# Adding the last square of thirteen norms on TensorE instead of VectorE

## The chip, the cores and the metric
The kernel runs on one core of a Trainium2 chip. A core has engines that work side by side, each with its own instruction stream: TensorE (PE in the rows; PEld is its weight load), VectorE (DVE), ScalarE (ACT), GpSimd (POOL), and SyncE (SP), which issues most transfers. The metric is the time of one execution in microseconds (us), as the device takes it.

## The reference
Two layers of a diffusion backbone work on 512 latent tokens of 1024 channels (and, in layer 0, on 256 context tokens as keys and values). Layer 0 mixes tokens by differential attention, layer 1 by a Hyena long convolution; a squared-ReLU MLP follows each. Every sub-layer has a norm over the channels before it and one behind it:

```
def rms_norm(x, g, eps=NORM_EPS):
    y = x * lax.rsqrt(jnp.mean(x * x, axis=-1, keepdims=True) + eps)
    return y * g

u = modulate(rms_norm(h, norm_mix_pre[i]), mod[0], mod[1])
y = mixer(u)                                   # attention or Hyena
h = h + mod[2] * rms_norm(y, norm_mix_post[i])
v = modulate(rms_norm(h, norm_mlp_pre[i]), mod[3], mod[4])
h = h + mod[5] * rms_norm(square(relu(v @ w_in)) @ w_out, norm_mlp_post[i])
```

## The kernel before, in words
Activations lie transposed: a tile has 128 channels on the partitions and tokens along its row, so 1024 channels are eight tiles. From the end of attention on, the tokens go in two halves of 256. Large products are split in three: a float32 operand becomes a rounded part (hh, uh, whi, wxhi) and a rest (hl, ul, wlo, wxlo), and each product is three matmuls, lines 308 to 310. The weights' parts are made on the chip: ScalarE casts a raw tile (line 286), VectorE or GpSimd subtracts (line 287).

A norm over channels for one half is this. As each of the eight tiles appears, ScalarE squares it (line 373, `nsq`, three buffers). `squares` adds them up: the sum with squares 2 to 5 on GpSimd, with 6 to 8 on VectorE (`NPOOL` = 5, line 382, `nacc`). `rstd` then sums over the partitions by TensorE: for each of the two blocks of 128 tokens a matmul whose loaded operand is the block of `nacc` and whose streamed one is a column of ones (line 349, into `ps_s`). A chain of small operations takes the inverse root: `rs_v` on VectorE (353), `rs_z` on ScalarE (329), five on VectorE (332 to 336). TensorE transposes the result to all partitions (line 362, `ps_bc`, "the broadcast"). It is used in one of two ways. `residual` multiplies y by it and adds the gain times y to the hidden state hT (lines 971 and 972, eight times each), and squares hT for the next norm as it goes. `prenorm` makes the modulated, split input of the next layer (lines 984 to 986, `nt`, `uh`, `ul`, eight times each).

There are fourteen such norms, counted here in order of time: 1 to 4 behind layer 0's attention (half 0: behind the mixer, before the MLP; then half 1 the same), 5 to 8 at the end of layer 0's MLP and before Hyena, 9 to 12 behind Hyena's output projection, 13 and 14 at the end of layer 1's MLP, one for each half. While a norm's chain runs, TensorE works on other matmuls of 256 columns of the other half or the next product (`ps_h`, in `halves`).

The last norm has a form of its own: `squares(..., two=True)` (set in `mlp`, line 1062, for layer 1's half 1) does not add the eighth square but returns the sum of seven and the eighth, and `rstd` runs a matmul for each of the two parts into the same column of `ps_s`.

The order of the instructions on each engine is not that of the code. A list scheduler places them by its own estimates of times and by priorities (`PRI`, by part of the program: `css` for the sum over channels, `cbc` for the broadcast, `res`, `pre`, `wload` and so on). A change of one instruction can so move others on all engines.

Of the kernel before, what the change touches and what calls it, by code (L numbers as in the profile page):

```python
# [20 lines left out]
KT = D // P  # L21
T = 512
TC = 256
HT = T // 2
# [232 lines left out]
class K:  # L257
# [104 lines left out]
                nc.tensor.transpose(bc[:, b * P:(b + 1) * P], z[:, b:b + 1].to_broadcast([P, P]), self.ident)  # L362
        return bc[:, 0:n]

    def squares(self, pool, n, two=False):


        nc = self.nc
        st = {"n": 0}

        def add(src):
            sq = pool.tile([P, n], F32, tag="nsq", name="nsq", bufs=3)
            nc.scalar.activation(sq, src, AF.Square)
            st["n"] += 1
            if st["n"] == 1:
                st["acc"] = sq
            elif two and st["n"] == KT:
                return st["acc"], sq
            else:
                eng = nc.vector if st["n"] > NPOOL else nc.gpsimd  # L380
                acc = pool.tile([P, n], F32, tag="nacc", name="nacc", bufs=2) if st["n"] == 2 else st["acc"]
                eng.tensor_add(acc, st["acc"], sq)
                st["acc"] = acc
            return st["acc"]
        return add
# [632 lines left out]
    def mlp(self, layer, u, after, chores=()):  # L1018

        nc, ap, y = self.nc, self.ap, self.y  # L1020
        uh, ul = u
        chores = iter(chores)
        for g in range(4):
            hid = [(self.hp.tile([P, T], F32R, tag="hh", name="hh"), self.hp.tile([P, T], F32R, tag="hl", name="hl"))
                   for _ in range(8)] if g == 0 else []
            if g == 0:
                ws = [self.wload(ap[f"w1_{layer}"][mt], f"w1f{layer}", True if layer else "xxxwwwxx"[mt])
                      for mt in range(8)]
                for h in range(2):
                    hs = slice(HT * h, HT * h + HT)  # L1030
                    yield h
                    self.halves(ws, lambda k: (uh[:, k], ul[:, k]),
                                lambda mt, ps: self.hidden(ps, hid[mt][0][:, hs], hid[mt][1][:, hs]), h,
                                HG[f"w1f{layer}"])
            else:
                for mt in range(8):
                    w = self.wload(ap[f"w1_{layer}"][8 * g + mt], f"w1_{layer}", True)
                    ps = self.pp.tile([P, T], F32, tag="mm", name="ps_1")
                    self.mm3(ps, [(*self.lin(w, k), uh[:, k], ul[:, k]) for k in range(KT)])
                    hid.append((self.hp.tile([P, T], F32R, tag="hh", name="hh"),  # L1040
                                self.hp.tile([P, T], F32R, tag="hl", name="hl")))
                    self.hidden(ps, *hid[mt])
                    next(chores, None)
            if g < 3:
                self.part = f"{layer}."
                for mt in range(8):
                    w = self.wload(ap[f"w2_{layer}"][g, mt], f"w2_{layer}", True)
                    ps = self.pp.tile([P, T], F32, tag="mm", name="ps_2")
                    self.mm3(ps, [(*self.lin(w, k), *hid[k]) for k in range(KT)])
                    if g == 0:  # L1050
                        nc.scalar.copy(y[:, mt], ps)
                    else:
                        nc.vector.tensor_add(y[:, mt], y[:, mt], ps)  # L1053
                    next(chores, None)
            else:
                for _ in chores:
                    pass
                self.part = "ef"[layer] + "."
                ws = [self.wload(ap[f"w2_{layer}"][g, mt], f"w2l{layer}", True) for mt in range(8)]
                for h in range(2):  # L1060
                    hs = slice(HT * h, HT * h + HT)
                    sq = self.squares(self.tp, HT, two=layer == 1 and h == 1)
                    res = {}

                    def evac(mt, ps):
                        nc.vector.tensor_add(y[:, mt, hs], y[:, mt, hs], ps)
                        res["acc"] = sq(y[:, mt, hs])
                    self.halves(ws, lambda k: hid[k], evac, h, HG[f"w2l{layer}"])
                    after(h, res["acc"])
# [280 lines left out]
```

## Time and profile before

| | |
|---|---|
| time, median of three runs | 1447.67 us (1447.07 to 1450.67) |
| the profiled execution: its time, its span | 1445.6 us, 1443.6 us |
| TensorE busy | 1390.7 us, 96% |
| VectorE busy | 922.8 us, 64% |
| ScalarE busy | 646.6 us, 45% |
| GpSimd busy | 181.6 us, 13% |

TensorE is busy for 90% or more of every slice of 36 us from the fourth of forty slices to the last but one. A row of a timeline below gives the start in us from the span's beginning, the busy time, engine, source line, operation, out<-in, shape and count of instructions that follow each other, and in brackets how long the engine had been idle before it and what ended that. Busy times of instructions that overlap are longer than the distance from one to the next; that distance is called the pitch here.

### The profile page before, as it was taken

To read this page: it belongs to the slowest core of one execution; us is meant where nothing else is said; L and a number is where in the kernel's file an instruction comes from. 1 tells how busy PE (TensorE), PEld (TensorE's weight loads), DVE (VectorE), ACT (ScalarE), POOL (GpSimd) and SP (SyncE) were. 2 spreads that over 40 slices of the span, in tenths; PEclk is the share of its full clock that TensorE was granted. 3 is DMA by queue.
4 is the path that set the end of the run, shared out by engine and by line. 5 is a ranking of instruction groups with operands and counts; after the bars stand their busy time and mean duration, and the time that the engine had idled before them with its cause. 6 is when DMAs were issued, how large, how long until landed. Compare 5 with 4: busy or idle time off the path is not lost.

```text
span 1443.6 us, 20833 instructions
## 1 busy us (share of the span) xinstructions
PE 1390.7 (96%) x8172; PEld 1190.3 (82%) x8172; DVE 922.8 (64%) x1572; ACT 646.6 (45%) x1120; POOL 181.6 (13%) x156
## 2 busy tenths in 40 slices
PE   7989999999999999999999999999999999999997
PEld 2378788888889988888788999888999788888897
DVE  5787988888577946646457586989687333242334
ACT  5345757477556543323223365434564433241332
POOL 0210101010002023040220211000020100101211
PEclk9999999999999999999999999999999999999999
DMA  8542132230144266645565026222322422222201
GB/s 297 223 156 89 67 116 81 74 110 22 44 151 143 95 221 224 211 153 175 189 204 175 30 89 204 98 93 88 103 89 74 146 96 95 98 92 102 88 30 59
DMA packets 56514, 176.66 MB, mean 122 GB/s; under 512 B 5728, under 2 KB 13024, under 8 KB 55904
## 3 DMA queue, kind: packets, MB, share of 16 engines
q1 hardware_dynamic: 54112, 166.94, 33.7%
q0 software_dynamic: 2304, 8.39, 1.6%
q8 instruction: 64, 1.05, 0.3%
q14 instruction: 34, 0.28, 0.1%
HBM read 169.02 MB, written 6.29 MB: 121 GB/s over the span
## 4 chain that ended last, share of the span: by engine, by line
PE 77%; DVE 8%; ACT 7%; DMA 4%; issue 2%; POOL 1%; SPq 0%; DVEq 0%; ACTq 0%; POOLq 0%
PE ps L309 11%; PE ps L310 11%; PE ps L308 11%; PE ps_h L308 5%; PE ps_h L310 5%; PE ps_h L309 5%; DMA mw<-in_wmod_dram 2%; ACT sw L743 2%; PE ps_z L308 2%; PE ps_z L310 2%; PE ps_z L309 2%; PE sc L877 1%; PE sc L878 1%; DMA raw<-in_w_dram 1%; PE ps_hf L603 1%
## 5 line engine op out<-in xcount | busy, mean ns | idle before, releaser
L286 ACT CAST whi<-raw 128x1024 fp32r<-128x1024 f32 x99 | 104.0, 1051 | 223.6 <-PE ps L309 87.7
L286 ACT CAST wxhi<-raw 128x1024 fp32r<-128x1024 f32 x92 | 96.6, 1050 | 210.2 <-PE ps L309 180.3
L287 DVE TENSOR_TENSOR wlo<-raw,whi 128x1024 fp32r<-128x1024 f32 x82 | 101.7, 1242 | 85.1 <-ACT whi L286 78.0
L287 DVE TENSOR_TENSOR wxlo<-raw,wxhi 128x1024 fp32r<-128x1024 f32 x69 | 84.4, 1224 | 85.5 <-ACT wxhi L286 84.2
L402 DVE SCALAR_TENSOR_TENSOR macc<-mw,silu,macc 128x1024 f32<-128x1024 f32 (+1 forms) x91 | 100.0, 1099 | 35.0 <-DMA mw<-in_wmod_dram 34.4
L310 PE MATMUL ps<-hh,wxlo 128*128 128x512 f32 x240 | 95.7, 399 | 0.0
L308 PE MATMUL ps<-hh,wxhi 128*128 128x512 f32 x240 | 95.5, 398 | 0.0
L309 PE MATMUL ps<-hl,wxhi 128*128 128x512 f32 x240 | 95.3, 397 | 0.0
L308 PE MATMUL ps<-uh,wxhi 128*128 128x512 f32 x240 | 94.2, 392 | 0.0
L309 PE MATMUL ps<-ul,wxhi 128*128 128x512 f32 x240 | 94.2, 392 | 0.0
L310 PE MATMUL ps<-uh,wxlo 128*128 128x512 f32 x240 | 93.9, 391 | 0.0
L287 POOL TENSOR_TENSOR wlo<-raw,whi 128x1024 fp32r<-128x1024 f32 x17 | 40.8, 2403 | 344.7 <-ACT whi L286 296.3
L1053 DVE TENSOR_TENSOR y<-y,ps 128x512 f32<-128x512 f32 x32 | 22.0, 686 | 88.1 <-PE ps L310 88.1
L286 ACT CAST hh<-relu 128x512 fp32r<-128x512 f32 (+1 forms) x80 | 42.0, 534 | 78.2 <-DVE relu L1015 78.0
L287 POOL TENSOR_TENSOR wxlo<-raw,wxhi 128x1024 fp32r<-128x1024 f32 x23 | 57.3, 2490 | 125.1 <-ACT wxhi L286 125.1
L883 ACT ACTIVATE p<-sc,mx 128x768 f32<-128x768 f32 x64 | 57.7, 904 | 27.4 <-DVE mx L881 24.1
L308 PE MATMUL ps_h<-uh,wxhi 128*128 128x256 f32 x240 | 66.9, 286 | 2.1 <-DVE relu L1015 1.4
L309 PE MATMUL ps_h<-ul,wxhi 128*128 128x256 f32 x240 | 67.8, 284 | 0.0
L310 PE MATMUL ps_h<-uh,wxlo 128*128 128x256 f32 x240 | 67.0, 283 | 0.0
L881 DVE TENSOR_REDUCE mx<-sc 128x1 f32<-128x768 f32 x64 | 60.8, 950 | 6.9 <-PE sc L878 6.3
L287 DVE TENSOR_TENSOR hl<-relu,hh 128x512 fp32r<-128x512 f32 (+1 forms) x80 | 47.5, 603 | 25.4 <-ACT hh L286 25.2
L820 POOL TENSOR_TENSOR lk<-rr,b 64x512 fp32r<-64x512 f32 x16 | 24.8, 1550 | 276.1 <-ACT b L818 246.1
(346 smaller groups left out, 4366.1 us busy)
## 6 DMA issues: line engine op xcount, KB each, us to landing
raw<-in_w_dram SPq DMA_DIRECT2D x128, 512.0 KB, 3.5
mw<-in_wmod_dram SPq DMA_DIRECT2D x72, 512.0 KB, 4.5
mw<-in_wmod_dram SPq DMA_DIRECT2D x48, 256.0 KB, 2.8
raw<-in_hin_dram SPq DMA_DIRECT2D x24, 512.0 KB, 3.5
raw<-in_wo_dram SPq DMA_DIRECT2D x11, 512.0 KB, 3.5
raw<-in_wq_dram SPq DMA_DIRECT2D x8, 512.0 KB, 3.4
raw<-in_wk_dram SPq DMA_DIRECT2D x8, 512.0 KB, 3.5
spec<-so POOLq DMA_DIRECT2D x8, 512.0 KB, 4.0
```

The source lines that it names most:

```text
L286: self.nc.scalar.copy(hi, src)
L287: (eng or self.nc.vector).tensor_sub(lo, src, hi.bitcast(F32))
L308: mm(ps, lhi, rhi, start=(start and i == 0), stop=False)
L309: mm(ps, lhi, rlo, start=False, stop=False)
L310: mm(ps, llo, rhi, start=False, stop=(stop and i == n - 1))
L402: nc.vector.scalar_tensor_tensor(acc, w, self.silu[:, kc:kc + 1], acc, op0=ALU.mult, op1=ALU.add)
L603: nc.tensor.matmul(pf, h2[:, i, tt * P:tt * P + P], fwo[:, gs], start=True, stop=True)
L743: nc.scalar.copy(sw[32 * (q ^ 1):32 * (q ^ 1) + 32, :], ps[32 * q:32 * q + 32, :])
L820: eng.tensor_sub(lk[hs_, s], src[hs_, :], b[hs_, s].bitcast(F32))
L881: nc.vector.tensor_reduce(mx, sc[:, 0:768], axis=AX.X, op=ALU.min)
L883: nc.scalar.activation(p, sc[:, 0:768], AF.Exp, scale=-1.0, bias=mx, accum_out=s1 if mp else s0[:, qb:qb + 1])
L1053: nc.vector.tensor_add(y[:, mt], y[:, mt], ps)
```

## The change
`squares` loses its argument `two`: it now always returns the sum of seven and the last square, so norms 1 to 13 get the form that the last norm has. Their eighth square is no longer added by VectorE; each block of 128 tokens gets a second matmul at line 349.

```
-    def squares(self, pool, n, two=False):
-
+    def squares(self, pool, n):
 ...
             if st["n"] == 1:
                 st["acc"] = sq
-            elif two and st["n"] == KT:
+            elif st["n"] == KT:
                 return st["acc"], sq
             else:
                 eng = nc.vector if st["n"] > NPOOL else nc.gpsimd
...
-                    sq = self.squares(self.tp, HT, two=layer == 1 and h == 1)
+                    sq = self.squares(self.tp, HT)
```

The scheduler places the instructions around the norms in another order; SyncE's stream stays as it was. From line 365 on, the changed kernel's lines are one lower than those of before.

VectorE at norm 6 (the first prenorm for Hyena), before: the chain from `rs_v` to `rs_z`, and what stands behind it. `wlo` and `wxlo` are weight splits of Hyena's input projection.

```order
L287 TENSOR_TENSOR wlo<-raw,whi 128x1024 x2
L353 TENSOR_SCALAR rs_v<-ps_s 128x2
L332 TENSOR_TENSOR rs_t<-rs_z 128x2
L333 TENSOR_TENSOR rs_t<-rs_t,rs_v 128x2
L334 TENSOR_SCALAR rs_q<-rs_t 128x2
L335 TENSOR_TENSOR rs_q<-rs_q,rs_t 128x2
L336 SCALAR_TENSOR_TENSOR rs_z<-rs_q,rs_z 128x2
L287 TENSOR_TENSOR wlo<-raw,whi 128x1024
L984 SCALAR_TENSOR_TENSOR nt<-hT,a_hy,ps_bc 128x256 x2
L287 TENSOR_TENSOR wxlo<-raw,wxhi 128x1024
L986 SCALAR_TENSOR_TENSOR ul<-nt,mod,uh 128x256 x2
```

The same place in the changed kernel:

```order
L287 TENSOR_TENSOR wlo<-raw,whi 128x1024 x2
L353 TENSOR_SCALAR rs_v<-ps_s 128x2
L287 TENSOR_TENSOR wlo<-raw,whi 128x1024
L332 TENSOR_TENSOR rs_t<-rs_z 128x2
L333 TENSOR_TENSOR rs_t<-rs_t,rs_v 128x2
L334 TENSOR_SCALAR rs_q<-rs_t 128x2
L287 TENSOR_TENSOR wxlo<-raw,wxhi 128x1024
L335 TENSOR_TENSOR rs_q<-rs_q,rs_t 128x2
L336 SCALAR_TENSOR_TENSOR rs_z<-rs_q,rs_z 128x2
L983 SCALAR_TENSOR_TENSOR nt<-hT,a_hy,ps_bc 128x256 x2
L985 SCALAR_TENSOR_TENSOR ul<-nt,mod,uh 128x256
```

Two weight splits that stood behind the chain now stand in it.

VectorE at the end of the residual of half 1, ahead of norm 8, before: `nacc` is the running sum of squares of hT.

```order
L971 TENSOR_TENSOR y<-y,ps_bc 128x256 x2
L972 SCALAR_TENSOR_TENSOR hT<-y,g_mlp_7593,hT 128x256 x2
L971 TENSOR_TENSOR y<-y,ps_bc 128x256 x2
L382 TENSOR_TENSOR nacc<-nacc,nsq 128x256
L972 SCALAR_TENSOR_TENSOR hT<-y,g_mlp_7593,hT 128x256 x2
L287 TENSOR_TENSOR wxlo<-raw,wxhi 128x1024
L382 TENSOR_TENSOR nacc<-nacc,nsq 128x256 x2
L287 TENSOR_TENSOR wxlo<-raw,wxhi 128x1024
L353 TENSOR_SCALAR rs_v<-ps_s 128x2
```

The same place in the changed kernel:

```order
L970 TENSOR_TENSOR y<-y,ps_bc 128x256 x2
L971 SCALAR_TENSOR_TENSOR hT<-y,g_mlp_7596,hT 128x256 x2
L970 TENSOR_TENSOR y<-y,ps_bc 128x256 x2
L381 TENSOR_TENSOR nacc<-nacc,nsq 128x256
L971 SCALAR_TENSOR_TENSOR hT<-y,g_mlp_7596,hT 128x256 x2
L983 SCALAR_TENSOR_TENSOR nt<-hT,a_hy,ps_bc 128x256
L381 TENSOR_TENSOR nacc<-nacc,nsq 128x256
L983 SCALAR_TENSOR_TENSOR nt<-hT,a_hy,ps_bc 128x256
L353 TENSOR_SCALAR rs_v<-ps_s 128x2
L985 SCALAR_TENSOR_TENSOR ul<-nt,mod,uh 128x256
```

One add and a weight split are gone ahead of `rs_v`, and two operations `nt` of half 0's prenorm, which stood ahead of the residual, now stand near its end.

TensorE at norm 8, before: `ps_h` with different numbers are different output tiles of Hyena's input projection for half 0.

```order
L309 MATMUL ps_h_8227<-ul_7653,wxhi_8106 128x256
L310 MATMUL ps_h_8227<-uh_7652,wxlo_8107 128x256
L308 MATMUL ps_h_8278<-uh_7652,wxhi_8112 128x256
L309 MATMUL ps_h_8278<-ul_7653,wxhi_8112 128x256
L349 MATMUL ps_s_7994<-ones_69,nacc_7962 128x1 x2
L310 MATMUL ps_h_8278<-uh_7652,wxlo_8113 128x256
L308 MATMUL ps_h_8278<-uh_7652,wxhi_8112 128x256
L309 MATMUL ps_h_8278<-ul_7653,wxhi_8112 128x256
```

The same place in the changed kernel:

```order
L308 MATMUL ps_h_8235<-uh_7656,wxhi_8114 128x256
L309 MATMUL ps_h_8235<-ul_7657,wxhi_8114 128x256
L310 MATMUL ps_h_8235<-uh_7656,wxlo_8115 128x256
L349 MATMUL ps_s_8000<-ones_69,nacc_7969 128x1
L349 MATMUL ps_s_8000<-ones_69,nsq_7998 128x1
L349 MATMUL ps_s_8000<-ones_69,nacc_7969 128x1
L349 MATMUL ps_s_8000<-ones_69,nsq_7998 128x1
L308 MATMUL ps_h_8130<-uh_7656,whi_8084 128x256
L308 MATMUL ps_h_8131<-uh_7656,whi_8090 128x256
L308 MATMUL ps_h_8132<-uh_7656,whi_8096 128x256
```

The sum has four matmuls in place of two. Between norm 7's broadcast and it there are 47 wide matmuls now, 76 before.

## Rows read from the trace of the kernel before

**Rows 1.** the page: busy time of the engines, and the chain by engine
```profile
PE 1390.7 (96%) x8172; PEld 1190.3 (82%) x8172; DVE 922.8 (64%) x1572; ACT 646.6 (45%) x1120; POOL 181.6 (13%) x156
...
PE 77%; DVE 8%; ACT 7%; DMA 4%; issue 2%; POOL 1%; SPq 0%; DVEq 0%; ACTq 0%; POOLq 0%
```

**Rows 2.** TensorE's waits from 430 us to the end: us in total, times, longest
```profile
PE ps_s L349 <- DVE nacc L382: 3.6, 4, 1.3
PE ps_bc L362 <- DVE rs_z L336: 2.5, 2, 1.6
PE ps_m L414 <- DVE macc L402: 1.7, 1, 1.7
PE ps_h L308 <- DVE relu L1015: 1.4, 2, 0.9
PE ps L308 <- ACT hh L286: 1.0, 2, 0.8
PE ps_s L349 <- ACT nsq L373: 0.9, 1, 0.9
```

**Rows 3.** VectorE in time, first norm: start, busy us, what [idle before]
```profile
438.07 1.48 DVE L382 TENSOR_TENSOR nacc<-nacc,nsq 128x256 f32<-128x256 f32 x3 [0.63 <-POOL nacc L382]
```

**Rows 4.** the line of the sum over channels: ns min/median/max, first, last
```profile
L349 PE MATMUL ps_s<-ones,nacc x56: 166/250/271, 439.6 to 1433.3; 128*128 128x1 f32 x56
```

**Rows 5.** TensorE in time at the first norm
```profile
439.61 0.60 PE L349 MATMUL ps_s<-ones,nacc 128*128 128x1 f32 x4 [1.31 <-DVE nacc L382]
440.07 0.36 PE L308 MATMUL ps_h<-hh,uh 128*128 128x256 f32 x1
440.28 0.28 PE L309 MATMUL ps_h<-hl,uh 128*128 128x256 f32 x1
```

**Rows 6.** TensorE in time at the last norm
```profile
1432.98 0.38 PE L349 MATMUL ps_s<-ones,nsq 128*128 128x1 f32 x2 [0.90 <-ACT nsq L373]
1433.22 0.36 PE L349 MATMUL ps_s<-ones,nacc 128*128 128x1 f32 x2
```

**Rows 7.** TensorE in time, layer 0's output projection
```profile
461.05 0.40 PE L362 MATMUL ps_bc<-vil,rs_z 128*128 128x128 f32 x2 [0.89 <-DVE rs_z L336]
...
481.20 0.39 PE L308 MATMUL ps_h<-uh,wxhi 128*128 128x256 f32 x1 [0.42 <-DVE relu L1015]
```

**Rows 8.** TensorE in time, end of layer 0's MLP into Hyena
```profile
811.96 0.58 PE L349 MATMUL ps_s<-ones,nacc 128*128 128x1 f32 x4 [0.52 <-DVE nacc L382]
...
827.86 0.25 PE L349 MATMUL ps_s<-ones,nacc 128*128 128x1 f32 x1
...
829.74 0.40 PE L362 MATMUL ps_bc<-vil,rs_z 128*128 128x128 f32 x2
...
844.11 0.38 PE L362 MATMUL ps_bc<-vil,rs_z 128*128 128x128 f32 x2
...
854.14 0.61 PE L349 MATMUL ps_s<-ones,nacc 128*128 128x1 f32 x4 [0.55 <-DVE nacc L382]
```

**Rows 9.** VectorE in time, the same stretch
```profile
842.03 0.47 DVE L984 SCALAR_TENSOR_TENSOR nt<-hT,a_hy,ps_bc 128x256 f32<-128x256 f32 x1
...
844.53 0.75 DVE L971 TENSOR_TENSOR y<-y,ps_bc 128x256 f32<-128x256 f32 x2
...
852.00 1.22 DVE L287 TENSOR_TENSOR wxlo<-raw,wxhi 128x1024 fp32r<-128x1024 f32 x1
853.14 0.95 DVE L382 TENSOR_TENSOR nacc<-nacc,nsq 128x256 f32<-128x256 f32 x2
```

**Rows 10.** ScalarE in time, the same stretch
```profile
828.98 1.05 ACT L286 CAST whi<-raw 128x1024 fp32r<-128x1024 f32 x1 [0.37 <-DMA raw<-in_hin_dram]
830.88 1.05 ACT L286 CAST wxhi<-raw 128x1024 fp32r<-128x1024 f32 x1 [0.85 <-DMA raw<-in_hin_dram]
```

**Rows 11.** TensorE in time, Hyena's output projection
```profile
1059.45 0.60 PE L349 MATMUL ps_s<-ones,nacc 128*128 128x1 f32 x4 [1.20 <-DVE nacc L382]
...
1086.13 0.35 PE L308 MATMUL ps_h<-uh,wxhi 128*128 128x256 f32 x1 [0.94 <-DVE relu L1015]
```

## The prediction

> **What bounds the kernel now.** I read the page first, then TensorE's own waits, then the stretches around the norms. The page gives PE 96% of the span against 64% for DVE, and PE 77% of the chain that ended last [rows 1]. So TensorE's instruction stream is the budget: what is added to it is paid, unless it falls into a moment in which TensorE would have stood still. How many such moments there are is the second view, TensorE's waits from 430 us to the end, the part in which all fourteen norms over channels lie [rows 2]. Its six largest rows come to 3.6 + 2.5 + 1.7 + 1.4 + 1.0 + 0.9 = 11.1 us in about 1014 us. Three of these belong to places that the change leaves alone: 1.7 us (a modulation sum), and 0.9 and 1.6 us in the last norm, which has the new form already. What is left is under 7 us. The reader should see from this that there is very little to win at the norms, and that a few tens of small matmuls are as large as the whole prize.
>
> **What the change removes and adds.** Thirteen norms lose one VectorE add each. Three adds in a row take 1.48 us [rows 3], so one is 0.5 us on an engine with 36% of its time free; what it is worth is only what TensorE waits for it. Each of these norms gains two matmuls of one column, one for each block of 128 tokens. The source line has 56 records for 14 norms x 2 blocks [rows 4], so a float32 matmul of one column is two records, and a norm gains four. Their price is read from their pitch, not from the 0.25 us of a record, because records overlap: four of them start at 439.61 and the next wide matmul starts at 440.07 [rows 5], so four cost 0.46 us. The last norm agrees: a pair starts at 1432.98 and the next at 1433.22, 0.24 us for two [rows 6]. A wide matmul starts 0.12 us after the one before, but the first one after a group comes 0.21 us after its predecessor (440.07, then 440.28); that 0.09 us exists already at each norm and comes again only where the new order splits a group. So the plain sum is 13 x 0.46 = 6.0 us of TensorE time.
>
> The trace's price for a one-column record is 0.115 us. The Trainium skill, "TensorE: Matmul & The Clock Gate", section "Back-to-back issue gap", gives about 60 cycles, 25 ns, for a matmul of 1 to 64 columns taken alone; by that the 52 records would be 1.3 us, an estimate, and the change would be free. The same page's section "LDWEIGHTS (loading the stationary operand)" goes by the columns of the operand that is loaded, and here each record loads a fresh block of 128 columns. The trace decides for the higher price.
>
> **Layer 0's output projection (norms 1 to 4).** Added: 4 x 0.46 = 1.8 us. At the first norm TensorE waits 1.31 us for the last add [rows 5]. The add's 0.5 us goes, but the new order issues the sum over channels four wide matmuls earlier (4 x 0.12 = 0.48 us), so the wait stays about as long. Later in the stage TensorE waits 0.89 us for the broadcast's input and 0.42 us for a squared ReLU [rows 7]; both are ends of VectorE's chain, which isn't later than before, so TensorE's extra work fits into them. 1.8 - 0.9 - 0.4 = +0.5 us.
>
> **End of layer 0's MLP into Hyena (norms 5 to 8).** Added: 1.8 us again. The 0.52 us wait at 811.96 [rows 8] shrinks by the saved add and grows by three matmuls that stand earlier: -0.2 us. Here the order changes most.
> - Norm 6: the chain of small VectorE operations behind the sum now has two weight splits of 1.22 us between its steps [rows 9], where before they stood behind it. They are not free to run early: their casts on ScalarE start when their transfers land, at 828.98 and 830.88, and take 1.05 us each [rows 10]. So the second split runs from about 832.0 to 833.1, and the broadcast can start about 833.6, not at 829.74 [rows 8]. TensorE now has 36 wide matmuls between sum and broadcast, not 12: it comes about 833.0 (827.86 + 0.8 for what was added before and here + 36 x 0.12). A wait of about 0.6 us replaces one of 0.09.
> - Norm 7: 40 matmuls lie ahead of its sum, its adds end within 0.3 us of TensorE's arrival: +0.1 us.
> - Norm 8: between the broadcast at 844.1 and the sum TensorE had 76 matmuls; in the new order 47. So it comes 29 x 0.12 = 3.5 us earlier, less about 0.3 us by which it is late: about 850.4, not 853.59. What it waits for is VectorE's residual: it starts at 844.53 and its last add ended about 854.1 [rows 9], 9.6 us. Without the weight split in it (1.14 us of pitch) and the last add (0.5), with one prenorm operation that now stands in it (0.4, the pitch of the row at 842.03), it is 8.4 us, from about 844.9: ready at 853.3. The wait is 2.9 us against 0.55 [rows 8], +2.3 us. The matmuls moved behind the sum are still to be done, so this isn't given back.
>
> Stage: 1.8 - 0.2 + 0.5 + 0.1 + 2.3 = +4.5 us. The trace shows none of these new waits, so they are bounded: norm 8's lies between 0 (VectorE's residual, the longest thing there, keeps up) and about 5 us (the residual starts 2 us later, because the broadcasts of norms 6 and 7 slide with their weights).
>
> **Hyena's output projection (norms 9 to 12).** Added 1.8 us. The 1.20 us wait at 1059.45 [rows 11] loses the add's 0.5 and TensorE's own 0.46 us of lateness, but the sum stands 9 matmuls earlier (+1.1): about 0.1 us longer or shorter, taken as -0.1. The wait of 0.94 us for a squared ReLU at 1086.13 [rows 11] takes up TensorE's later arrival, by half, since VectorE's chain is reordered there as well: -0.5. Sum +1.2 us.
>
> **Last MLP, half 0 (norm 13).** No wait there, +0.5 us.
>
> **Sum.** 0.5 + 4.5 + 1.2 + 0.5 = 6.7 us on the profiled execution's 1445.6 us: 1452.3. That execution is 2.07 us under the median of the runs shown (1447.67), so the forecast is 1447.67 + 6.7 = 1454.4 us, 0.46% slower. About 0.3% (4.3 us) is what a measurement of this kernel can tell from no change.
>
> **Rivals.**
> 1. The order at norms 6 to 8 doesn't hurt: VectorE's residual finishes as TensorE comes, or matmuls ahead of the sum are late anyway. For it: VectorE has one operation less in each norm, and its stage has idle time. Against it: 29 matmuls fewer stand ahead of norm 8's sum. Then the +2.3 and +0.5 go: 6.7 - 2.8 = 3.9, and with a little more taken up by waits about +3: 1450.7 us, within 0.3%.
> 2. Not slower: the shorter VectorE chain closes the waits of the norms. The four waits for the add are 3.6 us, the broadcast's 0.9, the ReLU's 1.4, the MLP's for its split input 1.0 [rows 2, 7]: 6.9 us against 6.0 added, -0.9 us, 1446.8. It decides this way only if at each of these places the end of the adds comes earlier by at least as much as TensorE does; against it stand the earlier places of the sums at norms 1, 8 and 10. A gain of over 0.3% would need 4.3 + 6.0 us of removed waits, more than there are.
> 3. Worse: the late broadcast of norm 6 carries through norms 7 and 8 (its weights' transfers bound it, 0.85 us of ScalarE's idle time shows that [rows 10]), and norm 8 waits 5 us in place of 2.9, norm 7 about 1: 6.7 + 3 = +9.7, 1457.4 us.
> 4. The small records cost next to nothing beside the wide ones. The pitch of 0.115 us would have to be the loading of a block that hides behind wide matmuls. Then 52 x 0.09 = 4.7 us go: +2.0, 1449.7 us. The four records at 439.61 and the wide one after them [rows 5] speak against it, since nothing overlaps there. The 25 ns of the skill's page would bear this rival out.
>
> **How the numbers follow.** My forecast gets 0.56, rival 1 0.22, rival 2 0.08, rival 3 0.11, rival 4 0.03. The forecast's own spread is 2 us either way, so 0.53 of its 0.56 lies beyond 4.3 us; with rival 3 that is 0.64 slower. Rivals 1, 2 and 4 and the rest are within 0.3%: 0.33. Faster by over 0.3% is left 0.03, for a cause that I don't see. The range runs from 1449.5 (rival 1 with its own spread) to 1458.5 us (most of rival 3).
>
> **What the changed profile would show.** The line of the sum over channels has 52 more records for the last square, at a pitch of about 0.115 us; VectorE has 13 adds fewer. TensorE's waits at this line at norm 8 are 2 to 3.5 us, now for the last square or the seventh add; at norm 6's broadcast about half a microsecond; those at 461.05 and 481.20 are nearly gone. Before 436 us nothing moves. It would be wrong if norm 8's sum shows no wait, if the four records cost under 0.2 us, or if the waits of [rows 2] fall by more than 4 us.

## The result and the profile after

The changed kernel takes 1458.78 us (median of four runs, 1455.24 to 1459.63) against 1447.41 us: a ratio of 1.0071 (95% interval 1.0056 to 1.0086), by which it is 10.3 us slower (8.1 to 12.4); the two medians themselves are 11.4 us apart. In a second measurement, with five runs, the ratio was 1.0073 (1.0061 to 1.0086). The forecast was 6.7 us slower: the right side, and two thirds of the size. The median lies 0.3 us above the upper end of the stated range, 1458.5 us; by the ratio, on the forecast's base of 1447.67 us, it is 1457.9 us and inside. Single executions of one kernel differ by some microseconds, so below the parts are read from stretches of the traces, and totals only with their intervals.

The profiled execution took 1458.62 us, its span is 1456.6 us, 13.0 us longer than before. The page's line of the engines:

```profile
PE 1400.4 (96%) x8224; PEld 1199.6 (82%) x8224; DVE 917.4 (63%) x1559; ACT 646.1 (44%) x1120; POOL 182.8 (13%) x156
```

TensorE's busy time rose by 9.7 us against [rows 1], VectorE's fell by 5. The line of the sum over channels now has 56 records for the last square, 52 more than before, and VectorE 28 adds of squares (13 fewer):

```profile
L349 PE MATMUL ps_s<-ones,nacc x56: 164/251/352, 437.0 to 1446.4; 128*128 128x1 f32 x56
...
L349 PE MATMUL ps_s<-ones,nsq x56: 164/250/352, 437.3 to 1446.6; 128*128 128x1 f32 x56
```
```profile
L381 DVE TENSOR_TENSOR nacc<-nacc,nsq 128x256 f32<-128x256 f32 x28 | 11.8, 422 | 15.8 <-POOL nacc L381 12.4 <-ACT nsq L372 2.9
```

TensorE's waits from 430 us on (us in total, times, longest), to be read against [rows 2]:

```profile
PE ps_s L349 <- DVE nacc L381: 6.5, 6, 3.1
PE ps_bc L362 <- DVE rs_z L336: 3.7, 4, 1.6
PE ps_m L413 <- DVE macc L401: 2.6, 1, 2.6
PE ps L308 <- ACT hh L286: 1.0, 1, 1.0
PE ps_s L349 <- ACT nsq L372: 0.9, 1, 0.9
PE ps_h L308 <- ACT nsq L372: 0.8, 1, 0.8
```

They did not shrink. The wait for the sum of squares, which the removed adds should have shortened, went from 3.6 to 6.5 us, and half of that is one wait of 3.1 us.

Where the time went, by the starts of the same TensorE instructions in both traces (the sum of a norm, or its broadcast):

| stretch | before, us | after, us | difference | forecast |
|---|---|---|---|---|
| start to the last sum of attention | 424.3 | 422.3 | -2.0 | 0 |
| from there to the first transposes of layer 0's MLP, into `ps_m` (norms 1 to 4) | 113.9 | 115.6 | +1.7 | +0.5 |
| from there to norm 5's sum (layer 0's MLP) | 273.8 | 275.5 | +1.7 | 0 |
| norm 5's sum to norm 9's (norms 5 to 8, then Hyena) | 234.5 | 243.5 | +9.0 | +4.5 |
| norm 9's sum to norm 13's | 365.4 | 367.5 | +2.1 | +1.2 |
| norm 13's sum to norm 14's broadcast | 23.6 | 24.2 | +0.6 | +0.5 |

The stretches without a changed norm come to -0.3 us. The first is shorter mainly since TensorE's clock fell at 388 us in the trace of before and not in this one. In layer 0's MLP the wait for the modulation sum (`ps_m`) was 2.6 us, not 1.7, and half clock (1.2 in place of 2.4 GHz) followed it here, from 791 to 795 us. One trace of each kernel can't say whether these two belong to the execution or to the change. The traces of all experiments below speak for the change: the fall at 388 us is in the four kernels without the new form at norms 1 to 13 (before, zero, noadd, warm6) and in one of the other nine (only6); half clock behind the modulation sum is in none of the four and in eight of the nine (all but fill7), and layer 0's MLP takes 273.4 to 274.4 us in the four and 275.3 to 277.3 in the nine. Only6, where no norm ahead of the sixth is changed, has 276.2. Why is open, and in the changed kernel's trace the two nearly cancel.

The four stretches with norms come to 13.4 us; the forecast gave them 6.7. How firm each is, the other traces show as well. From norm 9's sum to norm 13's five kernels without the new form there took 365.4 to 365.8 us (zero, with its added records, 368.0) and six with it 367.3 to 367.5 (fill7, with a wait of 1.1 us further on, 368.4). Norms 1 to 4 are less firm: 113.9 to 115.8 us in the five without it (115.2 in only6), 116.4 in zero and 115.6 to 116.7 in the seven with it.

The largest is norms 5 to 8. Norm 6 first: VectorE's chain behind the sum, with the two weight splits in it (start, busy us, what, idle before it):

```profile
830.68 0.16 DVE L353 TENSOR_SCALAR rs_v<-ps_s 128x2 f32<-128x2 f32 x1 [1.94 <-PE ps_s L349]
831.65 1.23 DVE L287 TENSOR_TENSOR wlo<-raw,whi 128x1024 fp32r<-128x1024 f32 x1 [0.81 <-ACT whi L286]
...
834.23 1.22 DVE L287 TENSOR_TENSOR wxlo<-raw,wxhi 128x1024 fp32r<-128x1024 f32 x1 [0.88 <-ACT wxhi L286]
...
835.56 0.16 DVE L336 SCALAR_TENSOR_TENSOR rs_z<-rs_q,rs_z 128x2 f32<-128x2 f32 x1
```

ScalarE's casts for these splits, and TensorE's broadcast behind the chain and sum of norm 7:

```profile
830.57 1.05 ACT L286 CAST whi<-raw 128x1024 fp32r<-128x1024 f32 x1 [2.15 <-DMA raw<-in_hin_dram]
...
833.15 1.05 ACT L286 CAST wxhi<-raw 128x1024 fp32r<-128x1024 f32 x1 [1.37 <-DMA raw<-in_hin_dram]
```
```profile
835.86 0.40 PE L362 MATMUL ps_bc<-vil,rs_z 128*128 128x128 f32 x2 [0.79 <-DVE rs_z L336]
...
841.50 0.35 PE L349 MATMUL ps_s<-ones,nacc 128*128 128x1 f32 x2 [0.45 <-DVE nacc L381]
```

The second cast waited 1.37 us for its transfer (0.85 in [rows 10]), the second split 0.88 us for the cast, and the chain that took 1.4 us before (from `rs_v` at 828.15 to the end of `rs_z`) takes 5. The broadcast came 6.1 us later than before (1.4 us of it stem from ahead of norm 5) and TensorE waited 0.79 us for it, then 0.45 us at norm 7.

Norm 8, TensorE and VectorE:

```profile
856.37 0.56 PE L349 MATMUL ps_s<-ones,nacc 128*128 128x1 f32 x2 [3.11 <-DVE nacc L381]
856.79 0.56 PE L349 MATMUL ps_s<-ones,nsq 128*128 128x1 f32 x2
...
858.07 0.99 PE L308 MATMUL ps_h<-uh,whi 128*128 128x256 f32 x3
```
```profile
847.67 0.75 DVE L970 TENSOR_TENSOR y<-y,ps_bc 128x256 f32<-128x256 f32 x2
...
855.41 0.47 DVE L983 SCALAR_TENSOR_TENSOR nt<-hT,a_hy,ps_bc 128x256 f32<-128x256 f32 x1
855.80 0.42 DVE L381 TENSOR_TENSOR nacc<-nacc,nsq 128x256 f32<-128x256 f32 x1
856.14 0.47 DVE L983 SCALAR_TENSOR_TENSOR nt<-hT,a_hy,ps_bc 128x256 f32<-128x256 f32 x1
```

TensorE waits 3.11 us for the seventh add, as the residual that starts at 847.67 ends. And something else is to be seen: two records start 0.42 us after the two before them. In [rows 5, 6] two took 0.23. The windows of that stretch (length, TensorE's busy time and records, granted clock, DMA share, GB/s) say why:

```profile
850.00:854.00 4.00, 3.26 (x28) 1.00 0.00 0
854.00:858.00 4.00, 1.63 (x8) 0.78 0.02 4
858.00:862.00 4.00, 4.00 (x19) 0.50 0.22 77
862.00:866.00 4.00, 4.00 (x32) 0.87 0.60 185
```

Behind the wait the granted clock is the lower of its two levels, 1.2 in place of 2.4 GHz, until about 863 us. The missing clock is 4 x (0.22 + 0.50 + 0.13) = 3.4 us of TensorE's time. So the stage's 9.0 us are 1.8 for the records, 3.5 more of waits (0.79 - 0.09, 0.45, 3.11 - 0.55, 0.35 - 0.52 at norm 5) and 3.4 of clock; 0.3 is left over, perhaps for groups that the new order splits, which is not shown.

In the other stages with norms no wait is long, and in sum they were not used up. From 436 to 540 us TensorE's waits were 4.1 us before and are 4.0 now:

```profile
PE ps_s L349 <- DVE nacc L381: 1.8, 2, 1.3
PE ps L308 <- ACT hh L286: 1.0, 1, 1.0
PE ps_bc L362 <- DVE rs_z L336: 0.7, 1, 0.7
PE ps_h L308 <- ACT uh L984: 0.5, 1, 0.5
```

At Hyena's output projection [rows 11] they were 2.1 us and are 2.1 now:

```profile
PE ps_h L308 <- ACT nsq L372: 0.8, 1, 0.8
PE ps_s L349 <- DVE nacc L381: 0.7, 1, 0.7
PE ps_bc L362 <- DVE rs_z L336: 0.6, 1, 0.6
```

### The profile page after: what moved, and what is told of

The parts are those of the page before. It is cut to its first block, busy times and chain, and to the rows that moved or that the text cites. A ratio compares the mean times of both kernels' runs of the same rounds, so it can differ in the third digit from the quotient of the medians.

```text
span 1456.6 us, 20918 instructions
## 1 busy us (share of the span) xinstructions
PE 1400.4 (96%) x8224; PEld 1199.6 (82%) x8224; DVE 917.4 (63%) x1559; ACT 646.1 (44%) x1120; POOL 182.8 (13%) x156
## 4 chain that ended last, share of the span: by engine, by line
PE 76%; DVE 9%; ACT 7%; DMA 5%; issue 2%; POOL 1%; SPq 0%; ACTq 0%; DVEq 0%; POOLq 0%
PE ps L309 11%; PE ps L310 11%; PE ps L308 11%; PE ps_h L308 5%; PE ps_h L310 4%; PE ps_h L309 4%; DMA mw<-in_wmod_dram 2%; ACT sw L742 2%; PE ps_z L310 2%; PE ps_z L308 2%; PE ps_z L309 2%; DMA raw<-in_w_dram 2%; PE ps_s L349 1%; PE sc L876 1%; PE sc L877 1%
## 5 line engine op out<-in xcount | busy, mean ns | idle before, releaser
L882 ACT ACTIVATE p<-sc,mx 128x768 f32<-128x768 f32 x64 | 57.7, 904 | 27.1 <-DVE mx L880 24.2
```

Source lines behind the costliest of these rows:

```text
L882: nc.scalar.activation(p, sc[:, 0:768], AF.Exp, scale=-1.0, bias=mx, accum_out=s1 if mp else s0[:, qb:qb + 1])
```

## The experiments

The theory after the result: the 52 records cost their full price (6 us), the adds were worth nothing, and the rest is the new order at norms 6 to 8, with the clock's fall that follows from it. The rival: the two-part form itself costs 10 us, spread over its norms. Every edit is made to the kernel before. In them, TWO is the set of the norms that have the new form (norm 14 always).

**Only norm 6, and all but norm 6.** The sets that have the new form are {6, 14} and all but 6:

```
+TWO = (6, 14)
...
-        acc = self.residual(y, acc, g0, 0, self.squares(self.tp, HT))
+        acc = self.residual(y, acc, g0, 0, self.squares(self.tp, HT, two=2 in TWO))
...                                     (the other calls of squares in the same way)
```

> Of the thirteen norms only norm 6 (half 0's prenorm for Hyena) gets the new form; the other twelve keep the add. The order around norms 6 to 8 is then close to that of the changed kernel: 38 wide matmuls between norm 6's sum and its broadcast, 49 between norm 7's broadcast and norm 8's sum (before: 13 and 76). Theory 1, the order and the clock: most of the loss comes from this one norm, +0.5 for four records, about +3.5 for TensorE's waits at norms 6 to 8 and about +3 for the half clock that follows the wait at norm 8: +6 to +7.5 us, and the granted clock of the stretch 850 to 870 shows the fall. Rival, the price of the matmuls spread over all norms (10 us over 13): +0.8 us, no fall of the clock.

Measured: 1.0053 (1.0035 to 1.0072), 7.7 us slower by a change whose records are 0.46 us. Norm 5's sum to norm 9's takes 242.6 us, 8.1 more than before. TensorE, and the window from 848 to 872 us (length; busy time and instructions of PE, PEld, DVE, ACT and POOL; granted clock, DMA share, GB/s), here and in the kernel before:

```profile
855.99 0.58 PE L310 MATMUL ps_h<-ul,whi 128*128 128x256 f32 x1 [3.38 <-DVE ul L987]
```
```profile
848.00:872.00 24.00, 20.59 (x146) 20.18 (x144) 17.21 (x41) 13.43 (x29) 3.38 (x4) 0.86 0.25 86
```
```profile
848.00:872.00 24.00, 23.45 (x196) 23.24 (x195) 14.76 (x36) 12.83 (x29) 2.35 (x3) 1.00 0.13 45
```

The wait is here for an input tile `ul` of Hyena's projection, ahead of norm 8's sum. Before, TensorE ran 196 matmul records in these 24 us; here it runs 146, at a mean clock of 0.86.

> The changed kernel with norm 6 alone in the old form. The order keeps 13 wide matmuls between norm 6's sum and broadcast and 78 between norm 7's broadcast and norm 8's sum, as before. Theory 1: about +4 us against the kernel before (12 x 0.46 = 5.5 less 1 to 2 taken up by waits), the waits at norm 8 under 1 us, no half clock there. Rival: twelve thirteenths of the loss stay, +9 to +10 us.

Measured: 1.0048 (1.0032 to 1.0064), 6.9 us: more than the theory's 4, less than the rival's 9 to 10; the interval, 4.6 to 9.3 us, leaves out the first and takes in the lower part of the second. The stage decides: 237.4 us, 2.9 more than before, and full clock:

```profile
848.00:872.00 24.00, 22.68 (x190) 22.48 (x189) 16.71 (x39) 13.55 (x31) 3.50 (x4) 1.00 0.16 58
```

So most of the stage's 9 us hangs on norm 6, as the theory had it. Of the 2.9 us, 1.4 are the records of three norms and 1.0 are waits, above all one of 1.32 us at 853.9 us for an input tile `ul` of Hyena's projection. The theory was too low elsewhere too: it took 1 to 2 us off the records for waits, and left out layer 0's MLP, 1.5 us longer than before in this trace.

**Norms 5 to 8 apart from the others.** Sets {5, 6, 7, 8, 14} and its complement.

> Norms 5 to 8 in the new form, all others in the old one; the order at norms 6 to 8 is that of the changed kernel (38 and 47 wide matmuls). Theory 1: this stage alone carries the 8.6 us that the two traces differ by between norm 5 and Hyena, the half clock after norm 8 included: +8 to +9 us, the clock of 856 to 863 at half. Rival, that the waits follow from the whole kernel's shifted times and not from this stage's order: under +5 us, no half clock there.

Measured: 1.0053 (1.0035 to 1.0071), 7.7 us, just under the 8 to 9 expected; stage 242.4 us (+7.9), with a wait of 3.13 us at norm 8 and half clock behind it. The new form of the other norms isn't needed for it.

> Norms 5 to 8 in the old form, 1 to 4 and 9 to 13 in the new one; the order of the old kernel is kept at norms 5 to 8. Theory 1: the parts that the profile of the changed kernel shows there, +1.7 (norms 1 to 4), +2.3 (9 to 12) and +0.4 (13), +4 to +4.5 us. Rival: nine thirteenths of the loss, +7 us.

Measured: 1.0027 (1.0013 to 1.0040), 3.9 us; the stage takes 235.4 us (+0.9) at full clock. That agrees with the 4 to 4.5 expected.

**The price of the records, and of the adds.** The first keeps all adds and gives norms 1 to 13 a tile of zeros as second part; the second leaves out the eighth square:

```
-            parts = sq if isinstance(sq, tuple) else (sq,)
+            parts = sq if isinstance(sq, tuple) else (sq, self.zsq) if nb == 2 and not self.at else (sq,)
```
```
+            elif st["n"] == KT:
+                return st["acc"]
```

> The kernel before, with all its adds, and in norms 1 to 13 a second matmul for each block whose loaded operand is a tile of zeros: the price of the 52 records alone, in nearly the old order (14 and 75 wide matmuls at norms 6 to 8). Theory 1: 52 x 0.115 = 6.0 us less what falls into TensorE's waits, +4 to +6 us, no wait at norm 8 beyond 1 us and no half clock in that stretch. Rival, that the records themselves cost the 10 us: +9 to +11 us. If they were 25 ns each: +1.3 us.

Measured: 1.0040 (1.0026 to 1.0054), 5.8 us (3.8 to 7.8): the plain sum is 6.0. The pitch at norm 8 is what the sum was made with, 0.23 us for two:

```profile
857.73 0.38 PE L350 MATMUL ps_s<-ones,nacc 128*128 128x1 f32 x2 [0.67 <-DVE nacc L383]
857.97 0.36 PE L350 MATMUL ps_s<-ones,zsq 128*128 128x1 f32 x2
858.20 0.36 PE L350 MATMUL ps_s<-ones,nacc 128*128 128x1 f32 x2
```

> The eighth square is left out of norms 1 to 13: neither VectorE nor TensorE adds it (13 adds fewer, no matmul more; part of the computation is missing). What VectorE's adds were worth at all. Theory 1 (TensorE's stream bounds, VectorE's adds only end a few waits): 0 to -2 us. Rival 2 of the prediction, that the shorter VectorE chain closes the norms' waits: -4 to -6 us.

Measured: 0.9997 (0.9988 to 1.0007), within 1.7 us of nothing. The thirteen adds on VectorE, 5.5 us at 0.42 us each, are worth nothing that can be measured when they are left out. The scheduler moved operations here too: its trace has a wait of 1.32 us for `ul` at 851 us that the trace of before hasn't, so the adds' own worth, in the old order, may be larger by about as much. That is far from the 6.9 us of removed waits that rival 2 of the prediction needs.

**What starves TensorE.** The two weight splits are held behind norm 6's chain on VectorE; the rest is as in the changed kernel:

```
-        ws = [self.wload(ap["hin"][i], "hin0", True) for i in first]
+        ws = []
+        for j, i in enumerate(first):
+            with self.tc.issue_after(self.rz6.ins) if j in (2, 3) else nullcontext():
+                ws.append(self.wload(ap["hin"][i], "hin0", True))
```

> All norms in the new form, but the two weight splits on VectorE that had moved into norm 6's chain are held behind it. 21 wide matmuls stand between norm 6's sum and broadcast (changed kernel 38, before 13) and 61 between norm 7's broadcast and norm 8's sum (47 and 78 to 76). Theory 1: the wait at norm 8 falls by 14 x 0.12 = 1.7 us to about 1.4, that at norm 6's broadcast to under 0.3, and the half clock of that stretch goes, 3 us more: +5 to +6 us against the kernel before, 5 less than the changed kernel. Rival, that the two-part form itself is the cost: +9 to +11 us still.

Measured: 1.0053 (1.0033 to 1.0072), 7.7 us, not 5 to 6; the stage takes 240.2 us. The wait at norm 8's sum and at norm 6's broadcast went, but not the half clock: TensorE now waits just ahead of the sum, for `ul`, an input tile of Hyena's projection, and the clock falls behind that wait.

```profile
855.47 0.38 PE L310 MATMUL ps_h<-ul,whi 128*128 128x256 f32 x1 [1.57 <-DVE ul L987]
```
```profile
848.00:872.00 24.00, 22.43 (x163) 22.22 (x162) 16.89 (x41) 14.39 (x32) 3.41 (x4) 0.86 0.18 62
```

The expectation was wrong in its cause: the place of norm 8's sum is not what matters. In the new order the last two of eight input tiles of half 0 (`nt` of tiles 6 and 7, the rows at 855.41 and 856.14 above) are made behind the residual of half 1 (in keep2 the last `ul` of both). The matmuls that need them can't run, and those that don't are used up. So the next edit makes these tiles first, by one edge on VectorE; in the kernel before they stand ahead of the residual without it [rows 9]:

```
         for k in range(KT):
-            nc.vector.tensor_mul(y[:, k, hs], y[:, k, hs], bc)
+            with self.tc.issue_after(self.last.ins) if k == 0 and h and self.part == "e." else nullcontext():
+                nc.vector.tensor_mul(y[:, k, hs], y[:, k, hs], bc)
```

> All norms in the new form; one edge more on VectorE: the residual of half 1 (behind norm 7) is issued behind the last operation of half 0's prenorm, as the old order had it. TensorE then has 96 wide matmuls between norm 7's broadcast and norm 8's sum (changed kernel 47, before 76); norm 6 is left as in the changed kernel (38). Theory, as it now stands: TensorE ran out of matmuls, since the input tiles 6 and 7 of half 0 were made behind the residual; with them made first, the wait of 3.1 us at norm 8 and the half clock behind it go. Norm 5's sum to norm 9's sum then takes 234.5 + 1.8 + 0.7 + 0.4 = 237.4 us, in place of 243.5; the time is +4 to +6 us against the kernel before, 4 to 6 under the changed kernel. Rival, that the shift of the sums at norm 6 or the two-part form makes the clock fall: stage over 241 us, time as the changed kernel's.

> The changed kernel again, on the same chip and beside the same runs as hold7, since single executions of one kernel differ by some us: +9 to +11 us against the kernel before, the half clock behind norm 8's wait there again.

Measured on one chip: hold7 1.0049 (1.0036 to 1.0061), 1454.85 us; the changed kernel again 1.0073 (1.0061 to 1.0086), 1458.82 us. The intervals just touch; the medians are 4.0 us apart, and every one of hold7's five times (1453.05 to 1457.11) is below every one of the other five (1457.86 to 1460.31). Against the kernel before hold7 is 7.1 us slower (5.2 to 8.8), where 4 to 6 were expected. The stage takes 238.2 us with the edge (237.4 expected) and 242.0 without it. At norm 8, hold7:

```profile
863.39 0.38 PE L350 MATMUL ps_s<-ones,nacc 128*128 128x1 f32 x2 [0.45 <-DVE nacc L383]
863.63 0.36 PE L350 MATMUL ps_s<-ones,nsq 128*128 128x1 f32 x2
```
```profile
848.00:872.00 24.00, 23.46 (x194) 23.03 (x194) 20.38 (x53) 15.62 (x35) 3.83 (x4) 1.00 0.28 88
```

and the changed kernel's second trace:

```profile
858.13 0.35 PE L349 MATMUL ps_s<-ones,nacc 128*128 128x1 f32 x2 [3.09 <-DVE nacc L381]
```
```profile
858.00:862.00 4.00, 3.87 (x25) 0.75 0.08 12
862.00:866.00 4.00, 4.00 (x30) 0.82 0.77 247
```

The same wait as in the first trace, 3.09 us, but the clock fell later, near 860 us, and for less: 4 x (0.25 + 0.18) = 1.7 us. The sum's records still ran at full clock, two in 0.22 us. So the order's waits are the same in both traces of this kernel, and what the clock adds behind them is not.

**The clock by itself.** The changed kernel with matmuls that nothing reads, ahead of norm 8's sum; and the kernel before with such matmuls where every trace so far shows an idle of 2.96 us and half clock behind it, at the first projection of the queries:

```
+                for _ in range(7):
+                    nc.tensor.matmul(pb[:, 256:512], self.ident, fill, start=True, stop=True)
```
```
+        for _ in range(6):
+            nc.tensor.matmul(pl[:, 256:512], self.ones, self.vil[:, 0:256], start=True, stop=True)
```

> The changed kernel with seven matmuls of 256 float32 columns added ahead of norm 8's sum, into a free part of its PSUM tile; nothing reads them. They only keep TensorE busy where it waited 3.1 us. If the half clock follows from that wait: the wait shrinks by what they take, the clock stays full from 850 to 870 and the time falls by 2.5 to 3.5 us against the changed kernel (about +7 us against the kernel before), although TensorE has more to do. Rival, that the clock falls for another cause, or that the wait costs only itself: time as the changed kernel's or longer, the half clock stays.

Measured: 1.0072 (1.0057 to 1.0088), the time of the changed kernel. The clock stayed full:

```profile
848.00:872.00 24.00, 22.87 (x179) 21.98 (x178) 19.12 (x46) 14.91 (x34) 3.21 (x4) 1.00 0.25 80
```

The stage takes 241.5 us, 2.0 less than in the changed kernel's first trace and 0.5 less than in its second, with 3.0 us more of matmuls (14 records at 0.215 us) in it. In all four traces with a wait of over 3 us at this place (the changed kernel twice, only6, only58), and in keep2's with one of 1.57, the clock fell; in the eight whose longest wait between norm 5's sum and norm 9's is 1.32 us or less, this one among them, it did not. At this place the fall goes with the idle engine. It is no rule for others: in the same trace of fill7 the modulation sum's wait of 2.93 us, at 793 us, was followed by full clock. The gain expected in the total (2.5 to 3.5 us under the changed kernel) is not there: the added matmuls take 3.0 us themselves.

> The kernel before with six float32 matmuls of 256 columns ahead of the first projection of the queries, where TensorE is idle for 2.96 us (up to 75.7 us) and then runs at half clock for about 6 us in every trace so far; nothing reads them. At 0.43 us each (seven in fill7) they fill 2.6 us. If the half clock follows from that wait: it goes there, -2.5 to -3.5 us against the kernel before. Rival, that the clock falls there for another cause: 0 to +0.5 us and half clock from 75 to 81 as before.

Measured: 0.9995 (0.9983 to 1.0006). The half clock from 75 to 81 us is gone, the time is not. First the windows of before, then those of warm6, then TensorE's waits in warm6:

```profile
76.00:80.00 4.00, 4.00 (x10) 0.50 0.34 137
80.00:84.00 4.00, 4.00 (x15) 0.79 0.00 0
```
```profile
76.00:80.00 4.00, 3.99 (x18) 1.00 0.32 131
80.00:84.00 4.00, 3.94 (x18) 1.00 0.00 0
```
```profile
PE ps_kc L309 <- DVE rr L748: 2.1, 1, 2.1
PE ps_v L309 <- DVE rr L748: 1.6, 1, 1.6
```

TensorE is up to 2.2 us ahead at 87 us, and waits it off for VectorE's rotary products (2.1 and 1.6 us; before, one wait of 1.7): from 91 us on the two traces are 0.25 us apart. At this place TensorE's clock is not on the path. No version measured here is faster than the kernel before by more than its interval.

## Why the prediction came out as it did

- **The plain sum, 6.0 us: right.** 5.8 us measured with the records alone, pitch 0.11 to 0.12 us. Rival 4 falls with it. The Trainium skill, "TensorE: Matmul & The Clock Gate", section "Back-to-back issue gap", gives 25 ns for a small matmul taken alone; that is not the price of these records. The Trainium skill, same page, section "LDWEIGHTS (loading the stationary operand)", has a load take the number of its columns divided by 1.2, in ns: 107 ns for 128, an estimate that agrees with the pitch measured here. That the load sets this pitch is argued; no run varies the loaded columns.
- **VectorE's adds are worth little: right,** more so than I had it; leaving them out changes the time by less than 1.7 us (noadd).
- **"TensorE's extra work fits into them" (layer 0, +0.5; Hyena's output, +1.2): wrong.** Measured +1.7 and +2.1, about the plain 1.8 both times; Hyena's figure is the firm one, since all traces kept bear it out, while norms 1 to 4 vary by as much from trace to trace. The waits of 0.89 and 0.42 us shrank or went [rows 7], and others came, of 0.55 us at norm 4's sum and 0.2 more at the MLP's input, with the same sum. My reason was that VectorE's chain is not later than before. But that chain begins with TensorE's own sum, so work added there delays the end of the chain along with TensorE; a wait takes up only work that doesn't lie on the chain that ends it. The runs show the sums of the waits; that this is the reason is argued.
- **Norms 6 to 8, the waits: right.** 0.79, 0.45 and 3.11 us, forecast 0.6, 0.1 and 2.9. They could be read from the order of the two kernels' instructions and from durations of the trace. The reason that I gave for norm 8, a sum that stands 29 matmuls earlier, was only half of it: with the sum later (keep2) the wait moved to an input tile; with the tiles first (hold7) it fell to 0.45 us.
- **The price of that wait: mis-sized.** I counted 2.3 us for the time that TensorE stands still and nothing for what follows. The clock behind it cost 3.4 us more in one trace and 1.7 in another. The trace of before had the pattern to be seen, at 75 us: 2.96 us idle, then half clock; I left it out of the sum, since all the norms' waits were short. The term for norms 5 to 8 was 4.5 us and measured 9.0 and 7.5.
- **Rivals.** Rival 3 named the size (1457.4 us) by another cause, later broadcasts; its waits did not come. Rival 1 (no wait at norm 8) and rival 2 (waits that close) did not occur.

With 1.8 for each of three stages, 0.5 for norm 13, the waits' 3.5 and 1.7 to 3.4 of clock the sum is 11 to 13 us; the interval of the measured 10.3, 8.1 to 12.4, takes in its lower half. The stretches without a changed norm are left out of it: they nearly cancel in this trace, and whether the 1.7 us of layer 0's MLP come with the change stays open.

## What to carry to other kernels

Where one engine's stream is nearly full, moving work to it from an engine with idle time costs its full pitch times its count, and the waits that it seems to fit into may end with a chain that it delays. Compare the scheduled order, not the diff: a change of half a microsecond at one norm moved two small operations behind a long block on another engine and starved the full one. And a wait of TensorE can cost more than its length, so look at the granted clock in the microseconds behind it, and ask whether TensorE is on the path there at all.

## What the runs showed of the hardware that was not expected

- Half clock came behind waits of 1.57 us (keep2, at 855 us) and 3.1 us; behind a wait of 1.25 us at norm 1 it came in the trace of hold7 (442 us) and not in that of the changed kernel. The wait of 1.6 us near 387 us is the same in all thirteen traces, and half clock followed it in five. Behind the modulation sum it followed a wait of 1.89 us (no6) and not one of 2.93 us (fill7). A trace of one execution does not tell what the next will pay.
- It need not start as the wait ends: in two traces of the same kernel with the same wait (3.11 and 3.09 us) it was there when TensorE resumed in the one, and came some 2 us later in the other.
- A float32 matmul of 256 columns that loads a fixed block was two records at 0.215 us, against 0.115 us for one of a single column, which loads a block of 128 columns as well. From 1 to 256 columns the pitch did not quite double.
